# Two transformer models on one core: the passages between projections reordered, two weight units freed earlier, a mixer's last branch in other PSUM banks

## The chip, the core and the metric

The kernel runs on one core of a Trainium2 chip. A core has four compute engines with an instruction queue each: TensorE (PE: matmuls and transposes, results in PSUM), VectorE (DVE), ScalarE (ACT) and GpSimd (POOL); SyncE (SP) issues most transfers. Each queue is in order: an instruction that waits holds back all behind it. The metric is the device time of one execution in microseconds (us), the median over several runs.

## The reference

256 tokens of width 1024 go through two layers of a first model (a mixer with four branches, a layer norm, then a dense feed-forward net in layer 0 and eight experts in layer 1, a layer norm), and then through two layers of a second model (RMS norm, attention in two kinds, RMS norm, SwiGLU, with shifts, scales and gates that come from a conditioning vector). Cut to what matters:

```python
for layer in range(2):                       # first model
    p_swa, p_rwkv, p_fox, p_dsa, p_gate = split_cols(x @ w_in, IN_GROUPS)
    ...
    for i, (o, w) in enumerate(zip((o_swa, o_rwkv, o_fox, o_dsa), w_rows)):
        merged = merged + sigmoid(gate_i) * (o @ w)
    x = layer_norm(ALPHA * x + merged @ w_out, g0, b0)
    y = swiglu(x, w1, w3, w2)  if layer == 0 else  moe_ffn(x, router_w, ...)
    x = layer_norm(ALPHA * x + y, g1, b1)
for l in range(2):                           # second model
    sh_a, sc_a, g_a, sh_f, sc_f, g_f = split(silu(c) @ w_mod[l] + b_mod[l])
    h = rms_norm(x, norm_mix[l]) * (1 + sc_a) + sh_a
    x = x + g_a * (attention(h @ w_in[l]) @ w_out[l])
    h = rms_norm(x, norm_ffn[l]) * (1 + sc_f) + sh_f
    x = x + g_f * ((silu(h @ w_gate[l]) * (h @ w_up[l])) @ w_down[l])
```

All of it is float32.

## The kernel before, in words

The tokens lie in two tiles t of 128. A float32 product is made of three matmuls in a reduced format (fp32r): each operand is split into a high part (a cast, on ACT) and a low part (the rest, a subtraction on DVE), and high·high, high·low and low·high are added in PSUM.

**Weights.** `Stream` brings every weight once, in program order, in units of up to 512 KB. SP issues the transfer of a unit into a raw buffer (L107; 4 of these, 9 from the experts on); `pump` casts one unit's high part on ACT (`wh`, L125) and, one unit later, subtracts its low part on DVE (`wl`, L114). There are 6 pairs of `wh` and `wl`; a new unit may be cast once fewer than 6 are unreleased, and `W.dn` counts those released. `take(n)` hands out the next n units, `W.done()` releases all that have been handed out.

**Order.** The order of each engine is fixed when the program is built. Background generators (transfers of constants, the modulation rows from `w_mod`, which ACT scales at L1709 and POOL adds) are interleaved by a model clock at each `tick`.

**PSUM.** Four banks are named `acc`, four `sm`. `out_proj` takes the four `acc` banks for its sums (two tiles t, two halves n of 512 columns). It goes through the nk units of the weight, both tiles for each; the last `tail` units are held together, all of them first for t=0, then for t=1, so that the first tile's sums end early. `mixer` calls it with 8 units and the default tail of 5; the second model's attention has tail 4 of its own.

**A mixer's last branch** (nb == 4): for each of four column groups c the branch product goes into an `acc` bank, DVE multiplies it by the gate and adds it up (L935, L936), ACT casts the high part `mh` (L940) and DVE subtracts the low part `ml` (L941). `mh` and `ml` are what `out_proj` multiplies by `w_out`.

**A passage** is what lies between the end of one projection and the start of the next: the residual update on the sums in PSUM, the norm, and the turn: 8 transposes of each tile on PE (L340) into `sm` banks, 4 high casts on ACT (L704) and 4 low subtractions on DVE (L744 for t=0, L750 for t=1) of each tile. `normed_T` writes it. A norm consists of `part` (update and statistics of one half, L2112 and L660, or L2219, L2220, L688 and ACT's L681), `stats`, `scale` and `shift` (L668 and L671 for the layer norm; the RMS norm's shift, L691, with a wait for POOL). For the RMS norm (`early`) the order is: t=0's sums, t=1's first half, t=0's shift and turn, t=1's second half, t=0's low parts, t=1's shift and turn, t=1's low parts. `mid` is a start on the next projection with the first tile alone, between the two tiles' transposes; it is used ahead of both attentions of the second model (r=0 and r=6) and both mixers. There are seven passages with a norm: after mixer 0, after the dense net, after mixer 1, after the experts (r=0, where the last layer norm is joined with the first RMS norm), and r=3, r=6 and r=9 in the second model.

## Time and profile before

| | us |
|---|---|
| median of 3 runs (2001.23 to 2015.73) | 2003.49 |
| the profiled execution | 2003.65 |
| its span in the trace | 2001.8 |
| PE busy | 1832.4 (92%) |
| DVE busy | 1446.5 (72%) |
| ACT busy | 1170.8 (58%) |

The granted clock of TensorE was 0.96 of full speed in the mean. In the page's 40 slices of some 50 us PE is busy 0.9 or more in most; it has 0.5 in the slice from about 1250 us, and 0.7 in those from 0, 300, 800, 1400 and 1750 us. A row of a timeline gives the start, the duration, the engine, the line and the operation; what stands in brackets is the time that the engine was idle before it, and what ended that idle time. PE's matmuls are pipelined, so a matmul's duration is longer than its distance to the next one.

### The profile page before, as it was taken

What the parts mean: (1) busy time and instruction counts of PE and PEld (TensorE: products, weight loads), DVE (VectorE), ACT (ScalarE), POOL (GpSimd) and SP (SyncE); (2) the same over time, 40 slices, a digit from 0 to 9 for tenths busy, and PEclk for the clock granted to TensorE, in tenths of its full rate; (3) what the DMA queues carried; (4) which work ended last, traced back from release to release, by engine and by line L of the source; (5) the groups of instructions that cost most, each with busy time, mean ns of one, the idle gap of its engine ahead of it and who ended that gap; (6) DMA issues with size and microseconds to landing.
All of it is one profiled execution on the core that took longest, in us unless ns stands there. A gap on an engine that the chain in (4) does not pass through costs nothing. (4 is left out here: it accounts for less than half of the span.)

```text
span 2001.8 us, 31995 instructions
## 1 busy us (share of the span) xinstructions
PE 1832.4 (92%) x11703; PEld 1625.0 (81%) x11703; DVE 1446.5 (72%) x2255; ACT 1170.8 (58%) x1875; POOL 468.0 (23%) x345
## 2 busy tenths in 40 slices
PE   7999987998899999799999999598799888978998
PEld 7899977987698999588888888486698876768998
DVE  5886776666688656788888888777566758857554
ACT  4465744666465564377777777366466655746443
POOL 0110252777530100100000000111246765113000
PEclk9999988999999999889999999798899998989999
DMA  7553575787864444679999999655378785436662
GB/s 218 152 155 106 173 250 186 261 278 243 268 179 140 136 127 137 208 237 334 365 326 352 327 353 354 233 190 161 76 267 281 253 305 191 148 126 210 196 194 95
DMA packets 287071, 440.08 MB, mean 220 GB/s; under 512 B 31764, under 2 KB 178304, under 8 KB 286904
## 3 DMA queue, kind: packets, MB, share of 16 engines
q1 hardware_dynamic: 281960, 428.29, 64.6%
q0 software_dynamic: 2912, 8.59, 1.6%
q8 instruction: 94, 1.54, 0.3%
q10 hardware_dynamic: 2032, 1.06, 0.2%
q14 instruction: 73, 0.60, 0.1%
HBM read 427.60 MB, written 9.75 MB: 218 GB/s over the span
## 5 line engine op out<-in xcount | busy, mean ns | idle before, releaser
L114 DVE TENSOR_TENSOR wl<-raw,wh 128x1024 fp32r<-128x1024 f32 (+2 forms) x694 | 875.9, 1303 | 175.5 <-ACT wh L125 170.5
L125 ACT CAST wh<-raw 128x1024 fp32r<-128x1024 f32 (+2 forms) x694 | 695.4, 1030 | 201.4 <-PE sm L336 61.0
L336 PE MATMUL acc<-wh,b 128*128 128x512 f32 (+1 forms) x1232 | 417.2, 408 | 22.3 <-DVE b L935 10.5
L336 PE MATMUL sm<-b,wh 128*128 128x256 f32 x2112 | 378.1, 283 | 0.9 <-ACT wh L125 0.9
L336 PE MATMUL acc<-b,wh 128*128 128x256 f32 x2048 | 368.2, 283 | 0.2 <-DVE b L416 0.2
L1711 POOL TENSOR_TENSOR b<-b,b 128x512 f32<-128x512 f32 x168 | 309.8, 1844 | 228.5 <-ACT b L1709 215.5
L336 PE MATMUL sm<-wh,b 128*128 128x512 f32 (+1 forms) x1120 | 342.0, 382 | 0.0
L336 PE MATMUL sm<-b,wl 128*128 128x256 f32 x1056 | 302.2, 286 | 38.2 <-DVE wl L114 38.2
L336 PEld LDWEIGHTS sm<-b,wh 128*128 128x128 f32 x2112 | 332.1, 194 | 4.8 <-ACT wh L125 1.4
L336 PEld LDWEIGHTS acc<-b,wh 128*128 128x128 f32 x2048 | 312.5, 189 | 8.7 <-issue 7.3
L336 PEld LDWEIGHTS acc<-wh,b 128*128 128x128 f32 x1232 | 240.5, 196 | 82.2 <-DVE b L935 13.6
L336 PE MATMUL acc<-b,wl 128*128 128x256 f32 x1024 | 286.1, 279 | 3.0 <-DVE wl L114 3.0
L336 PE MATMUL acc<-wl,b 128*128 128x512 f32 (+1 forms) x616 | 248.6, 404 | 4.3 <-DVE wl L114 4.3
L336 PEld LDWEIGHTS sm<-b,wl 128*128 128x128 f32 x1056 | 205.4, 195 | 44.7 <-DVE wl L114 44.6
L336 PEld LDWEIGHTS sm<-wh,b 128*128 128x128 f32 x1120 | 209.8, 189 | 35.0 <-issue 0.2
L1709 ACT ACTIVATE b<-b,ccol 128x512 f32<-128x512 f32 x192 | 137.4, 724 | 151.8 <-DMA b<-in_w_mod_dram 151.8
L336 PE MATMUL sm<-wl,b 128*128 128x512 f32 (+1 forms) x560 | 213.5, 381 | 0.0
L336 PEld LDWEIGHTS acc<-b,wl 128*128 128x128 f32 x1024 | 193.5, 189 | 3.6 <-DVE wl L114 3.6
L336 PEld LDWEIGHTS acc<-wl,b 128*128 128x128 f32 x616 | 120.8, 196 | 30.5 <-DVE wl L114 7.5
L553 POOL TENSOR_TENSOR ln_mv<-ln_mv,mhalf 128x1 f32<-128x1 f32 x8 | 7.5, 932 | 525.4 <-DVE ln_mv L664 525.4
L336 PEld LDWEIGHTS sm<-wl,b 128*128 128x128 f32 x560 | 105.9, 189 | 18.2 <-DVE wl L114 0.5
L340 PE MATMUL sm<-ident,b 128*128 128x128 f32 (+1 forms) x242 | 46.9, 339 | 72.6 <-DVE b L691 32.1
(333 smaller groups left out, 1738.7 us busy)
## 6 DMA issues: line engine op xcount, KB each, us to landing
raw<-in_exp_w_dram SPq DMA_DIRECT2D x216, 512.0 KB
raw<-in_w_in_dram SPq DMA_DIRECT2D x152, 512.0 KB
b<-in_w_mod_dram SPq DMA_DIRECT2D x192, 256.0 KB
raw<-in_ffn_w_dram SPq DMA_DIRECT2D x66, 512.0 KB
raw<-in_exp_w_dram SPq DMA_DIRECT2D x64, 384.0 KB
raw<-in_w_gate_dram SPq DMA_DIRECT2D x44, 512.0 KB
raw<-in_w_up_dram SPq DMA_DIRECT2D x44, 512.0 KB
raw<-in_w_down_dram SPq DMA_DIRECT2D x44, 512.0 KB
```

The source lines that it names most:

```text
L114: self.K.nc.vector.tensor_sub(*self.lows.pop())
L125: nc.scalar.copy(wh[:, :w], raw[:, :w])
L336: return self.nc.tensor.matmul(out, lhsT, rhs, start=start, stop=stop)
L340: r = self.nc.tensor.transpose(out, in_, ident)
L553: self.nc.gpsimd.tensor_tensor(ap, ap, self.mhalf[:, :n], op=OP.pow)
L1709: nc.scalar.activation(r, r, AF.Copy, scale=cc[:, k : k + 1])
L1711: nc.gpsimd.tensor_add(w["a"], w["a"], r)
```

## The change

- In a mixer's last branch the product goes into `sm` banks, and `ml` of a column group is issued one group later (`last`).
- `out_proj`'s default tail is 4. During t=1's pass over the tail, after the unit at `tail - 3`, two units are declared released (`W.dn = W.ti - 2`) and `pump` casts one more; the same ahead of the last `ffn_down` of a feed-forward net.
- `normed_T`: sums and statistics of both tiles come first. For the RMS norm the shifts of t=0 and t=1 both stand behind t=1's sums; for the layer norm t=0's shift stays ahead of t=1's sums. All eight low parts come after both tiles' turns. `turn` is parted into `turn` (transposes) and `high`.
- At r=0 the joined norm uses the same order, and `mid` is left out there; it stays at r=6 and, with 456 columns, ahead of the mixers.

```diff
--- before.py
+++ after.py
@@ -612,7 +612,7 @@
                 self.tick()
         return ps
 
-    def out_proj(self, aT, nk, tail=5, split_at=None):
+    def out_proj(self, aT, nk, tail=4, split_at=None):
 
         ps = [[self.acc() for _ in range(2)] for _ in range(NT)]
 
@@ -640,6 +640,9 @@
                 part(t, nk - tail + j, w)
                 if t == 0:
                     self.tick()
+                elif j == tail - 3:
+                    self.W.dn = self.W.ti - 2
+                    self.W.pump()
             for n in range(2):
                 for j, w in enumerate(ws[-2:]):
                     part(t, nk - 2 + j, w, (n,))
@@ -692,13 +695,19 @@
 
         return part, stats, scale, shift
 
-    def turn(self, xT, x, t, lows):
+    def turn(self, x):
+
+        r = []
+        for g in range(2):
+            r.append(self.sm().rearrange("p (a b) -> p a b", a=4))
+            for j in range(4):
+                self.tr(r[g][:, j], x[g][:, j * P : (j + 1) * P], self.ident)
+        return r
+
+    def high(self, xT, pss, t, lows):
 
         sl = (slice(None), slice(None), slice(t * P, (t + 1) * P))
-        for g in range(2):
-            ps = self.sm().rearrange("p (a b) -> p a b", a=4)
-            for j in range(4):
-                self.tr(ps[:, j], x[g][:, j * P : (j + 1) * P], self.ident)
+        for g, ps in enumerate(pss):
             for a in range(2):
                 hi, lo = xT[0][2 * g + a][sl], xT[1][2 * g + a][sl]
                 self.nc.scalar.copy(hi, ps[:, 2 * a : 2 * a + 2])
@@ -707,46 +716,39 @@
     def normed_T(self, src, norm=None, early=False, mid=None):
 
 
+
         nc = self.nc
         xT = self.new_xT()
-        lows = ([], [])
+        lows = []
         rest = None
         if norm:
             part, stats, scale, shift = norm
-            for n in range(2):
-                part(0, n)
-                if early:
-                    scale(0, n)
-            stats(0)
+            for t in range(NT):
+                for n in range(2):
+                    part(t, n)
+                    if early and not t:
+                        scale(t, n)
+                if early and t:
+                    for n in range(2):
+                        scale(t, n)
+                stats(t)
+                if not early:
+                    for n in range(2):
+                        scale(t, n)
+                if not early and t == 0:
+                    for n in range(2):
+                        shift(t, n)
             if early:
-                part(1, 0)
-            else:
                 for n in range(2):
-                    scale(0, n)
-            for n in range(2):
-                shift(0, n)
-        self.turn(xT, src[0], 0, lows[0])
-        if mid:
-            rest = mid(xT)
-        if norm:
-            if early:
-                scale(1, 0)
-            else:
-                part(1, 0)
-            part(1, 1)
-            if early:
-                scale(1, 1)
-            stats(1)
-            if not early:
-                for n in range(2):
-                    scale(1, n)
-        for o in lows[0]:
-            nc.vector.tensor_sub(*o)
+                    shift(0, n)
+        self.high(xT, self.turn(src[0]), 0, lows)
         if norm:
             for n in range(2):
                 shift(1, n)
-        self.turn(xT, src[1], 1, lows[1])
-        for o in lows[1]:
+        if mid:
+            rest = mid(xT)
+        self.high(xT, self.turn(src[1]), 1, lows)
+        for o in lows:
             nc.vector.tensor_sub(*o)
         return (xT, rest) if mid else xT
 
@@ -917,8 +919,9 @@
             nb += 1
             rows = range(off[b], off[b + 1])
             ws = self.W.take(len(rows))
+            last = None
             for c in range(4):
-                ps = self.acc().rearrange("p (a b) -> p a b", a=2)
+                ps = (self.acc() if nb < 4 else self.sm()).rearrange("p (a b) -> p a b", a=2)
                 for j in range(2):
                     s = slice(c * 256 + j * P, c * 256 + (j + 1) * P)
                     for r, (wh, wl) in zip(rows, ws):
@@ -938,8 +941,14 @@
                     mh.append(self.b2(dt=F32R))
                     ml.append(self.b2(dt=F32R))
                     nc.scalar.mul(mh[c], mt[c], 0.5)
-                    nc.vector.scalar_tensor_tensor(ml[c], mt[c], 0.5, mh[c], op0=OP.mult, op1=OP.subtract)
-                    del mt[c]
+                    if last:
+                        last()
+
+                    def last(c=c, m=mt.pop(c)):
+                        nc.vector.scalar_tensor_tensor(ml[c], m, 0.5, mh[c], op0=OP.mult, op1=OP.subtract)
+
+            if last:
+                last()
             for r in sorted({r // 2 for r in rows}):
                 oh.d.pop(r), ol.d.pop(r)
         self.phase("w_out")
@@ -1342,6 +1351,8 @@
                 self.ffn_down(y, hid.pop(p - 1), self.W.take(2), p == 1, True)
         ws = self.W.take(4)
         self.ffn_down(y, hid.pop(np_ - 2), ws[:2], False, False)
+        self.W.dn = self.W.ti - 2
+        self.W.pump()
         self.ffn_down(y, hid.pop(np_ - 1), ws[2:], False, False, True)
         self.W.done()
         return y
@@ -2166,23 +2177,18 @@
                 hs = [[self.b2((P, 512)) for _ in range(2)] for _ in range(NT)]
                 part, stats, scale, shift = self.rms_norm(x, hs, update, pre["rows"])
                 if r == 0:
-                    def between(t, n, part=part, scale=scale):
-                        if t == 0:
-                            part(t, n)
-                        elif n == 0:
+                    def late(t, n, part=part, scale=scale):
+                        if t == 1 and n == 0:
                             for m in range(2):
                                 ln[2](1, m)
-
-                    def late(t, n, part=part, scale=scale):
-                        if t == 1:
-                            part(t, n)
-                        scale(t, n)
-
-                    norm = between, stats, late, shift
+                        part(t, n)
+
+                    norm = late, stats, scale, shift
                 else:
                     norm = part, stats, scale, shift
-                xT = self.normed_T(hs, norm, True, self.nat_start(512) if half == 0 else None)
-                if half == 0:
+                xT = self.normed_T(hs, norm, True, self.nat_start(512) if r == 6 else None)
+                begun = None
+                if r == 6:
                     xT, begun = xT
                 for t in range(NT):
                     self.store_x(xd, x, t)
```

The engines' new order is what the diff doesn't show. In the changed kernel the lines are shifted: L935, L936, L940 and L941 are L938, L939, L943 and L948; L2112 is L2123; L660 is L663; L2219 and L2220 are L2225 and L2226; the RMS norm's L688, L684 and L691 are L691, L687 and L694; L744 and L750 are one line, L752.

DVE, last branch of mixer 0, column groups c=0 to 2, before (`b_613` and `b_620` are `ml` of c=0 and c=1, `wl_3385` and `wl_3414` low parts of `w_out`'s units):

```order
L935 SCALAR_TENSOR_TENSOR b_550_2970<-b_550_2970,acc_3371 128x512
L936 TENSOR_TENSOR b_393_2144<-b_393_2144,b_550_2970 128x512
L941 SCALAR_TENSOR_TENSOR b_613_3397<-b_393_2144,b_612_3396 128x512
L114 TENSOR_TENSOR wl_3385<-raw_3253,wh_3384 128x1024
L935 SCALAR_TENSOR_TENSOR b_562_3049<-b_562_3049,acc_3400 128x512
L936 TENSOR_TENSOR b_402_2186<-b_402_2186,b_562_3049 128x512
L941 SCALAR_TENSOR_TENSOR b_620_3426<-b_402_2186,b_619_3425 128x512
L114 TENSOR_TENSOR wl_3414<-raw_3293,wh_3413 128x1024
L935 SCALAR_TENSOR_TENSOR b_579_3155<-b_579_3155,acc_3429 128x512
```

and now:

```order
L938 SCALAR_TENSOR_TENSOR b_550_2970<-b_550_2970,sm_3371 128x512
L939 TENSOR_TENSOR b_393_2144<-b_393_2144,b_550_2970 128x512
L114 TENSOR_TENSOR wl_3385<-raw_3253,wh_3384 128x1024
L938 SCALAR_TENSOR_TENSOR b_562_3049<-b_562_3049,sm_3399 128x512
L939 TENSOR_TENSOR b_402_2186<-b_402_2186,b_562_3049 128x512
L948 SCALAR_TENSOR_TENSOR b_613_3397<-b_393_2144,b_612_3396 128x512
L114 TENSOR_TENSOR wl_3413<-raw_3293,wh_3412 128x1024
L938 SCALAR_TENSOR_TENSOR b_579_3155<-b_579_3155,sm_3428 128x512
L939 TENSOR_TENSOR b_406_2206<-b_406_2206,b_579_3155 128x512
L948 SCALAR_TENSOR_TENSOR b_620_3425<-b_402_2186,b_619_3424 128x512
```

The low part of c=0 moved from behind its own sums, ahead of a weight's low part, to behind the sums of c=1; the reads are from `sm` banks.

DVE, ahead of the first layer norm, from the low part of a `w_out` unit to the first tile's update and statistics, before (`wl_3575` is the last unit of `w_out`):

```order
L114 TENSOR_TENSOR wl_3537<-raw_3417,wh_3536 128x1024
L114 TENSOR_TENSOR wl_3559<-raw_3446,wh_3558 128x1024
L114 TENSOR_TENSOR wl_3575<-raw_3505,wh_3574 128x1024
L2112 SCALAR_TENSOR_TENSOR b_631_3475<-b_631_3475,acc_3491 128x512
L660 BN_STATS ln_bs_3654<-b_631_3475 128x6
L2112 SCALAR_TENSOR_TENSOR b_632_3476<-b_632_3476,acc_3492 128x512
```

and now (`wl_3577` is the last unit of `w_out`):

```order
L114 TENSOR_TENSOR wl_3577<-raw_3505,wh_3576 128x1024
L114 TENSOR_TENSOR wl_3599<-raw_3532,wh_3598 128x1024
L114 TENSOR_TENSOR wl_3608<-raw_3553,wh_3607 128x1024
L2123 SCALAR_TENSOR_TENSOR b_631_3475<-b_631_3475,acc_3491 128x512
L663 BN_STATS ln_bs_3664<-b_631_3475 128x6
L2123 SCALAR_TENSOR_TENSOR b_632_3476<-b_632_3476,acc_3492 128x512
L663 BN_STATS ln_bs_3664<-b_632_3476 128x6
```

Two low parts of the next net's units (`wl_3599`, `wl_3608`) stand ahead of the first tile's update.

DVE in the passage r=3, from the first tile's shift to the second's, before (L691 is the shift, L744 the first tile's low parts):

```order
L691 SCALAR_TENSOR_TENSOR b_4305_19275<-b_4305_19275,rms_st_19279,rw_18986 128x512
L691 SCALAR_TENSOR_TENSOR b_4306_19276<-b_4306_19276,rms_st_19279,rw_18987 128x512
L688 TENSOR_TENSOR b_4307_19277<-b_4234_18972,rw_18982 128x512
L2219 TENSOR_TENSOR b_4324_19322<-acc_18993,b_4237_18979 128x512
L2220 TENSOR_TENSOR b_4235_18973<-b_4235_18973,b_4324_19322 128x512
L688 TENSOR_TENSOR b_4308_19278<-b_4235_18973,rw_18983 128x512
L684 SCALAR_TENSOR_TENSOR rms_st_19280<-rms_st_19280 128x1
L744 TENSOR_TENSOR b_4315_19285<-sm_19307,b_4311_19281 128x2x128
L744 TENSOR_TENSOR b_4316_19286<-sm_19307,b_4312_19282 128x2x128
L744 TENSOR_TENSOR b_4317_19287<-sm_19314,b_4313_19283 128x2x128
L744 TENSOR_TENSOR b_4318_19288<-sm_19314,b_4314_19284 128x2x128
L691 SCALAR_TENSOR_TENSOR b_4307_19277<-b_4307_19277,rms_st_19280,rw_18986 128x512
```

and now, from t=1's residual on (L694 is the shift):

```order
L2226 TENSOR_TENSOR b_4234_18972<-b_4234_18972,b_4324_19307 128x512
L2225 TENSOR_TENSOR b_4325_19311<-acc_18993,b_4237_18979 128x512
L2226 TENSOR_TENSOR b_4235_18973<-b_4235_18973,b_4325_19311 128x512
L691 TENSOR_TENSOR b_4310_19283<-b_4234_18972,rw_18982 128x512
L691 TENSOR_TENSOR b_4311_19284<-b_4235_18973,rw_18983 128x512
L687 SCALAR_TENSOR_TENSOR rms_st_19286<-rms_st_19286 128x1
L694 SCALAR_TENSOR_TENSOR b_4308_19281<-b_4308_19281,rms_st_19285,rw_18986 128x512
L694 SCALAR_TENSOR_TENSOR b_4309_19282<-b_4309_19282,rms_st_19285,rw_18987 128x512
L694 SCALAR_TENSOR_TENSOR b_4310_19283<-b_4310_19283,rms_st_19286,rw_18986 128x512
L694 SCALAR_TENSOR_TENSOR b_4311_19284<-b_4311_19284,rms_st_19286,rw_18987 128x512
L752 TENSOR_TENSOR b_4318_19291<-sm_19321,b_4314_19287 128x2x128
```

The first tile's shift moved from ahead of the second tile's last sums to behind them, and no low part stands between the two tiles' shifts.

## Rows read from the trace of the kernel before

**Rows 1.** page, part 1: engine, busy us (share of the span), instructions
```profile
PE 1832.4 (92%) x11703; PEld 1625.0 (81%) x11703; DVE 1446.5 (72%) x2255; ACT 1170.8 (58%) x1875; POOL 468.0 (23%) x345
```

**Rows 2.** waits of PE: who waited for whom, us in total, times, longest
```profile
PE sm L340 <- DVE b L691: 32.1, 8, 13.1
PE sm L340 <- DVE b L671: 14.6, 4, 5.0
...
PE acc L336 <- DVE b L935: 10.5, 6, 3.3
```

**Rows 3.** timeline of DVE, last branch: start us, us, engine, line, operation [idle before]
```profile
270.27 0.67 DVE L935 SCALAR_TENSOR_TENSOR b<-b,acc 128x512 f32<-128x512 f32 x1
270.98 0.69 DVE L936 TENSOR_TENSOR b<-b,b 128x512 f32<-128x512 f32 x1
272.37 0.69 DVE L941 SCALAR_TENSOR_TENSOR b<-b,b 128x512 fp32r<-128x512 f32 x1 [0.70 <-ACT b L940]
272.98 1.22 DVE L114 TENSOR_TENSOR wl<-raw,wh 128x1024 fp32r<-128x1024 f32 x1
```

**Rows 4.** timeline of PE, same columns, from that branch to the first LN's end
```profile
279.12 0.80 PE L336 MATMUL acc<-wh,b 128*128 128x512 f32 x1 [3.30 <-DVE b L935]
...
311.14 1.97 PE L340 MATMUL sm<-ident,b 128*128 128x128 f32 x8 [4.38 <-DVE b L671]
...
315.77 0.58 PE L336 MATMUL sm<-b,wl 128*128 128x256 f32 x1 [2.45 <-DVE wl L114]
```

**Rows 5.** timeline of ACT, same columns, in the first mixer's w_out
```profile
291.37 0.73 ACT L1709 ACTIVATE b<-b,ccol 128x512 f32<-128x512 f32 x1 [4.56 <-DMA b<-in_w_mod_dram]
```

**Rows 6.** timeline of SP, same columns: the queue that issues the transfers
```profile
285.10 0.33 SPq L107 DMA_DIRECT2D raw<-in_w_out_dram  x1
```

**Rows 7.** timeline of DVE from w_out's last lows to the first LN's second shift
```profile
293.06 3.80 DVE L114 TENSOR_TENSOR wl<-raw,wh 128x1024 fp32r<-128x1024 f32 x2 [4.08 <-ACT wh L125]
297.68 0.69 DVE L2112 SCALAR_TENSOR_TENSOR b<-b,acc 128x512 f32<-128x512 f32 x1 [0.82 <-PE acc L336]
...
304.55 0.69 DVE L2112 SCALAR_TENSOR_TENSOR b<-b,acc 128x512 f32<-128x512 f32 x1 [1.00 <-PE acc L336]
...
309.01 1.41 DVE L744 TENSOR_TENSOR b<-sm,b 128x256 fp32r<-128x256 f32 x4
310.34 1.41 DVE L671 SCALAR_TENSOR_TENSOR b<-b,ln_mv,b 128x512 f32<-128x512 f32 x2
```

**Rows 8.** windows: stretch, us, PE PEld DVE ACT POOL busy, PEclk, DMA share, GB/s
```profile
284.00:297.00 13.00, 12.24 (x48) 9.56 (x47) 8.70 (x6) 8.17 (x12) 6.95 (x4) 0.89 1.00 329
1276.80:1293.90 17.10, 5.70 (x16) 4.03 (x16) 13.46 (x23) 5.37 (x12) 2.47 (x3) 0.50 0.88 305
1437.20:1444.10 6.90, 3.86 (x17) 3.58 (x17) 5.45 (x13) 3.25 (x8) 6.08 (x12) 0.51 0.60 159
```

**Rows 9.** timeline of ACT at the second mixer's w_out
```profile
818.57 0.25 ACT L415 CAST rt_wh<-rt_w 128x64 fp32r<-128x64 f32 x1 [5.63 <-DMA rt_w<-in_router_w_dram]
```

**Rows 10.** timeline of DVE in the passage after the experts (r=0)
```profile
1285.16 1.41 DVE L691 SCALAR_TENSOR_TENSOR b<-b,rms_st,rw 128x512 f32<-128x512 f32 x2
...
1291.94 0.75 DVE L671 SCALAR_TENSOR_TENSOR b<-b,ln_mv,b 128x512 f32<-128x512 f32 x1
...
1296.26 1.41 DVE L691 SCALAR_TENSOR_TENSOR b<-b,rms_st,rw 128x512 f32<-128x512 f32 x2
```

**Rows 11.** timeline of PE in the same passage, both tiles' transposes
```profile
1286.06 1.94 PE L340 MATMUL sm<-ident,b 128*128 128x128 f32 x8 [13.09 <-DVE b L691]
...
1297.06 1.80 PE L340 MATMUL sm<-ident,b 128*128 128x128 f32 x8 [2.90 <-DVE b L691]
```

**Rows 12.** page, part 5: costliest groups: busy us, mean ns | idle before
```profile
L125 ACT CAST wh<-raw 128x1024 fp32r<-128x1024 f32 (+2 forms) x694 | 695.4, 1030 | 201.4 <-PE sm L336 61.0
```

**Rows 13.** timeline of PE in the passage r=3, second transposes and first projection
```profile
1440.07 1.94 PE L340 MATMUL sm<-ident,b 128*128 128x128 f32 x8 [4.24 <-DVE b L691]
...
1444.66 0.39 PE L336 MATMUL sm<-b,wl 128*128 128x256 f32 x1 [0.74 <-DVE wl L114]
```

## The prediction

> **What bounds the kernel now.** I read the page's busy times first: PE is busy 92% of the span, DVE 72%, ACT 58% [rows 1], so PE sets the time wherever it is fed, and only what makes PE wait, or lets its clock fall, can be won. The list of PE's waits says where: transposes that wait for DVE's shift, 32.1 us at the RMS norms and 14.6 us at the layer norms, and the branch products that wait for DVE to empty an `acc` bank, 10.5 us [rows 2]. Together that is 57 us, all of it at the places of the change. The timelines of DVE and PE at these places then show what DVE does in that time, and the windows with the granted clock show what PE does after it: 17.1 us at half speed around the long wait at r=0, 6.9 us after the shorter one at r=3 [rows 8].
>
> **Mixer 0 and its layer norm.** Four column groups cost DVE one `ml` each, and each of these waits 0.70 us for ACT [rows 3]. With `ml` one group later the four waits go: 4 x 0.70 = 2.8 us off the end of the last `ml`. The first `ml` moves the other way: it now stands behind a weight's low part (1.22), a sum (0.67) and an addition (0.69), less the wait of 0.70 [rows 3], so 1.9 us later. `out_proj` needs it in its third matmul, and PE waits there. This wait takes the place of the one for the bank, 3.30 us [rows 4], which the `sm` banks remove; I count the two, with the smaller bank waits, as part of the 2.8 and not again.
>
> What follows is a chain through the transfers. SP issues `w_out`'s last unit at 285.10 [rows 6], when DVE's low part behind the last `ml` has freed its raw buffer; 2.8 us earlier is the most. ACT then stands 4.56 us at a transfer of `w_mod` until 291.37 [rows 5], the two last casts behind it, and the low parts end at 293.06 + 3.80 = 296.86 [rows 7]. If all of it moves by 2.8 us, they end at 294.1. Then come the two new low parts, 2 x 1.22 = 2.4, so t=0's update starts at 296.5 and not at 297.68 [rows 7]. A tile takes 304.55 - 297.68 less the idle 1.00, that is 5.87 us [rows 7]; t=1's update starts at 302.4, 2.2 us earlier. The shorter tail lets PE keep up: six matmuls fewer stand behind the last unit. Behind t=1's sums, t=0's low parts go from between (310.34 - 309.01 = 1.33) [rows 7], and the wait of 2.45 us for a weight at the first matmul of the net goes [rows 4], since that weight is now ready. Sum: 2.2 + 1.3 + 2.45 = **-6.0**. The first term hangs on transfers: the DMA engines are busy all of 284 to 297, at 329 GB/s [rows 8], and the two units are 1 MB more, an estimate of 3.2 us at that rate. With nothing won there and the new low parts in full, it is +2.4 + 0.0 - 3.8 = -1.4; with the whole idle time of the transposes, 4.38 [rows 4], in place of the 2.2, it is -8.1.
>
> **The dense net's passage.** Only the low parts leave the path, 1.33 as in [rows 7], and one weight's low part comes ahead: **-1.5**, from -0.5 to -3.
>
> **Mixer 1 and its layer norm.** The same edits, but ACT waits 5.63 us for the router's weights until 818.57 [rows 9], and `w_out`'s casts are behind it. The transfer of these comes from SP behind the norm's rows and hangs little on `ml`, so what the four groups win is waited away there. What is left: the low parts, 1.33, and the tail. In 284 to 297 PE had 48 matmuls in 12.24 us [rows 8], 0.255 each; six fewer are 1.5, of which the two new low parts on DVE take some: I take 1.0. **-2.3**, from 0 to -5.
>
> **r=0.** Before, 1296.26 - 1285.16 = 11.1 us lie between the two tiles' shifts [rows 10], because two low parts for `mid` stand between. Now t=1's scale and part come ahead: from 1291.94 to 1296.26, less the low parts 1.33, is 3.0 us, so t=0's shift starts at 1288.2, t=1's 1.3 later at 1289.5. The second tile is ready 6.8 us earlier, but the eight matmuls of `mid`, done in the gap before, are still to do, the first weights are cast only behind the eight high parts on ACT, and the clock is low until 1293.9 [rows 8]. I place the projection's start at 1295: shift and transposes end by 1289.5 + 1.4 + 1.9 = 1292.8 [rows 10, 11], then come a cast (1.03) [rows 12] and a low part (1.22) [rows 3]. Before, the eight matmuls were done by the end of the second transposes, 1297.06 + 1.80 = 1298.9 [rows 11], and the high parts came behind that. Now they are still to do from 1295 on: 0.255 us each at a clock of 0.89 [rows 8] is 0.45 at half speed, 3.6 for the eight, so PE is at the same state at 1298.6. That is -0.3, and with the high parts done earlier as well I take **-1.0**, from +1 to -3.
>
> **r=3 and r=9.** They repeat each other to a tenth of a us. t=1's transposes at 1440.07 [rows 13] follow a shift that loses the low parts ahead of it, 1.33 as in [rows 7], and the wait of 0.74 for a weight [rows 13] goes, as one more is ready: -2.0. Against it, t=0's transposes now come directly ahead of t=1's, at half speed 1.94 for the eight [rows 13], and ACT has all eight high parts in a row: +0.4. **-1.6 each**, from -0.5 to -2.5.
>
> What the row shows here is a PE that waits 4.24 us [rows 13] between two short bursts and is then at half speed for 6.9 us [rows 8]. The Trainium skill, "TensorE: Matmul & The Clock Gate", section "HAM oscillation — how this bites in real kernels", says that idle gaps in PE's work should be kept short, since a long one drops the clock and every return to work is then paid at half rate again. This change makes one idle stretch out of two, which that rule speaks against. By the rule the two places would cost some us and not win them, by the rows, where the clock was low there already, they win 1.6 each.
>
> **r=6.** `mid` stays. One weight's low part, 1.22 as in [rows 3], and t=0's low parts, 1.33 as in [rows 7], leave the way of t=1's shift: -2.5. But t=0's transposes, and `mid` behind them, wait for t=1's sums, and t=1's transposes stand behind `mid` on PE. **-0.7**, from +1.5 to -2.5.
>
> **The rest** of the program keeps its order; at its start there is no norm and at its end no turn. Sum: 6.0 + 1.5 + 2.3 + 1.0 + 2 x 1.6 + 0.7 = 14.7 us. Against the profiled execution, 2003.65 (span 2001.8 and 1.85 around it), that is 1988.95. The profiled execution lies 0.16 above the median of the runs shown, so the forecast is **1989**.
>
> **Rivals.** *Weights late.* The units freed early land too late, and DVE, in order, stands at their low parts with the first tile's update behind them. For it speaks the DMA share of 1.00 [rows 8]; against it, that they come right behind `w_out`'s last unit in SP's queue. It costs the first term of mixer 0 and 1.0 at mixer 1: 14.7 - 4.6 - 1.0 = 9, so 1995.
>
> *Clock.* With the waits shorter, PE stays at full speed through more of the passages. Each stretch of 6.9 us [rows 8] that vanishes gives back half; four of them, at r=3, r=6, r=9 and one layer norm, are 14 more: 1975. Against it, at the RMS norms the idle time becomes one piece, and that no shorter by much than the 4.24 us of before [rows 13].
>
> *Slower.* At the RMS norms t=0's transposes wait for t=1's sums, and PE stands idle in one piece. If PE then stays low as long as at r=0, 17.1 and not 6.9 us [rows 8], r=3, r=6 and r=9 lose half of 10.2 each, 15.3, and the wait for the first `ml` comes on top, 2 x 1.9: 1989 + 19 = 2008. The gain is gone once these passages together stay at half speed for 29 us more (2 x 14.7). Against it: the wait of 13.09 us that went ahead there [rows 11] is three times as long as the 4.24 at r=3 [rows 13]. The rule of the Trainium skill named above ("TensorE: Matmul & The Clock Gate", "HAM oscillation — how this bites in real kernels") would make this the likelier outcome.
>
> **The numbers.** About 1% (20 us) is what a measurement of this kernel can tell from no change: faster means below 1983.5, slower above 2023.5. The forecast case (1981 to 1996) has 0.55; weights late, 0.20; the clock, 0.15; slower, 0.10. From the best ends of the forecast's terms and the clock case comes the low end, 1975; the high end takes in weights late with the passages' poor ends, 2001. Below it lie some 0.08, above it 0.10. Faster by over 1%: 0.14 of the clock case and 0.16 of the forecast's, whose terms' best ends together reach 1977, so 0.30. Slower by over 1% needs the slower case with more than its worked-out price: 0.06. Within 1%: 0.64.
>
> **What would show it.** In the changed kernel's profile: no wait of PE for DVE's product in the last branches, and one of about 1.9 us for the first `ml`; t=1's shift at r=3 and r=9 directly behind t=0's; no wait for a weight at the first matmul after mixer 0's norm, r=3 and r=9; the router's wait unchanged. The prediction is wrong if the first tile's update after mixer 0 starts later than before, if the half-speed stretches at r=3 and r=9 get much longer or vanish, or if the stage behind r=3, where ACT waits for `w_mod`, takes its gain back.

## The result and the profile after

The changed kernel takes 1983.32 us (median of 5 runs, 1982.3 to 1988.47), the kernel before 2005.3 us in the runs beside it: a ratio of 0.989, interval 0.9858 to 0.9922, so 22 us less. Of the five runs of the kernel before one, 2111.68 us, was a slow one, and the ratio leaves it out. The forecast was 1989, the range 1975 to 2001; against the 2003.49 us of the forecast's table the time lies just beyond the 1% bound, on the faster side. The profiled execution has a span of 1981.4 us, 20.4 less than before's.

The page's first part after, to be held against [rows 1], and PE's waits (who for whom, us in total, times, longest) against [rows 2]; L694 is the old L691, L674 the old L671, L948 the last branch's `ml`:

```profile
PE 1819.1 (92%) x11703; PEld 1618.3 (82%) x11703; DVE 1449.0 (73%) x2255; ACT 1169.1 (59%) x1875; POOL 471.0 (24%) x345
```

```profile
PE sm L340 <- DVE b L694: 30.9, 4, 16.1
...
PE sm L340 <- DVE b L674: 12.3, 4, 4.3
...
PE acc L336 <- DVE b L948: 2.5, 2, 1.6
```

The reader is to see two things. The same 11703 matmuls keep PE busy for 13.3 us less than in [rows 1]. That is not less work: summed over the stretches of low clock, PE was busy at half speed for 98 us and not 119, which accounts for some 10 of the 13.3, and only some 7 of the 20.4 us are idle time. How a gain divides between the two hangs on the execution: pin_all below, as fast in its profiled run (1982.74 us), has PE busy for 1826.7 us, 110 of them at half speed. And the list of waits hardly shows the gain: the RMS norms wait 30.9 us in four pieces in place of 32.1 in eight.

Mixer 0's tail and its norm. DVE (start, duration, operation, idle before), against [rows 3] and [rows 7]:

```profile
270.16 0.68 DVE L938 SCALAR_TENSOR_TENSOR b<-b,sm 128x512 f32<-128x512 f32 x1
...
273.94 0.69 DVE L948 SCALAR_TENSOR_TENSOR b<-b,b 128x512 fp32r<-128x512 f32 x1
...
280.03 1.47 DVE L948 SCALAR_TENSOR_TENSOR b<-b,b 128x512 fp32r<-128x512 f32 x2
...
291.82 1.53 DVE L114 TENSOR_TENSOR wl<-raw,wh 128x1024 fp32r<-128x1024 f32 x1 [4.07 <-ACT wh L125]
...
296.79 0.68 DVE L2123 SCALAR_TENSOR_TENSOR b<-b,acc 128x512 f32<-128x512 f32 x1
...
302.51 0.68 DVE L2123 SCALAR_TENSOR_TENSOR b<-b,acc 128x512 f32<-128x512 f32 x1
...
308.23 2.73 DVE L752 TENSOR_TENSOR b<-sm,b 128x256 fp32r<-128x256 f32 x8
```

ACT there, against [rows 5]:

```profile
290.13 0.72 ACT L1720 ACTIVATE b<-b,ccol 128x512 f32<-128x512 f32 x1 [4.77 <-DMA b<-in_w_mod_dram]
```

PE there, against [rows 4]:

```profile
274.68 0.73 PE L336 MATMUL acc<-wh,b 128*128 128x512 f32 x2 [1.63 <-DVE b L948]
...
291.84 0.49 PE L336 MATMUL acc<-wh,b 128*128 128x512 f32 x1 [2.46 <-ACT wh L125]
293.40 0.51 PE L336 MATMUL acc<-wl,b 128*128 128x512 f32 x1 [1.07 <-DVE wl L114]
...
307.79 1.69 PE L340 MATMUL sm<-ident,b 128*128 128x128 f32 x8 [4.31 <-DVE b L674]
```

The first `ml` is waited for 1.63 us (1.9 forecast), the last unit's low part ends at 293.35 (294.1), the first tile's update starts at 296.79 (296.5) and the second's at 302.51 (302.4). No weight is waited for at the net's first matmul.

One link is off. ACT's wait for `w_mod` ends at 290.13 for 291.37, 1.24 us earlier and not 2.8. The low parts end early all the same because only one of `w_out`'s, and not two as in [rows 7], stands behind that wait. And at `w_out`'s last unit PE waits 2.46 + 1.07 us, where it waited 0.76 before:

```profile
296.91 0.50 PE L336 MATMUL acc<-wl,b 128*128 128x512 f32 x1 [0.76 <-DVE wl L114]
```

The passages r=0, r=3 and r=6 on PE, against [rows 11] and [rows 13]:

```profile
1272.01 3.65 PE L340 MATMUL sm<-ident,b 128*128 128x128 f32 x16 [16.05 <-DVE b L694]
...
1420.60 3.46 PE L340 MATMUL sm<-ident,b 128*128 128x128 f32 x16 [3.54 <-DVE b L694]
...
1647.40 1.97 PE L340 MATMUL sm<-ident,b 128*128 128x128 f32 x8 [7.78 <-DVE b L694]
```

Before, the first tile's transposes at r=3, and both tiles' at r=6, were:

```profile
1434.54 1.29 PE L340 MATMUL sm<-ident,b 128*128 128x128 f32 x8 [0.89 <-DVE b L691]
...
1663.93 1.38 PE L340 MATMUL sm<-ident,b 128*128 128x128 f32 x8 [2.49 <-DVE b L691]
...
1670.60 1.97 PE L340 MATMUL sm<-ident,b 128*128 128x128 f32 x8 [3.43 <-DVE b L691]
```

At r=3 one wait of 3.54 us stands where 0.89, 4.24 and 0.74 stood. Windows of the changed kernel with the granted clock (us, busy times, clock, DMA share, GB/s), against [rows 8]:

```profile
1260.40:1284.30 23.90, 10.14 (x30) 8.02 (x31) 22.82 (x39) 11.69 (x23) 5.60 (x8) 0.50 0.86 300
1420.80:1424.30 3.50, 3.50 (x19) 3.34 (x18) 3.40 (x9) 2.15 (x7) 3.50 (x8) 0.51 0.62 225
```

The low stretch at r=3 is 3.5 us and not 6.9, but PE's busy time in it is 3.50 and not 3.86 [rows 8]; at r=0 it is 23.9 and not 17.1 and 3.4.

### The profile page after: what moved, and what is told of

Read it like the earlier page. It is cut to its first block, busy times and chain, and to the rows that moved or that the text cites. A ratio compares the mean times of both kernels' runs of the same rounds, so it can differ in the third digit from the quotient of the medians.

```text
span 1981.4 us, 32010 instructions
## 1 busy us (share of the span) xinstructions
PE 1819.1 (92%) x11703; PEld 1618.3 (82%) x11703; DVE 1449.0 (73%) x2255; ACT 1169.1 (59%) x1875; POOL 471.0 (24%) x345
## 3 DMA queue, kind: packets, MB, share of 16 engines
q10 hardware_dynamic: 2032, 1.06, 0.2%
## 5 line engine op out<-in xcount | busy, mean ns | idle before, releaser
L336 PE MATMUL sm<-b,wh 128*128 128x256 f32 x2176 | 384.8, 281 | 2.0 <-ACT wh L125 2.0
L336 PE MATMUL acc<-b,wh 128*128 128x256 f32 x1984 | 357.1, 283 | 0.2 <-DVE b L416 0.2
L336 PEld LDWEIGHTS sm<-b,wh 128*128 128x128 f32 x2176 | 338.0, 192 | 5.9 <-ACT wh L125 2.8
L336 PE MATMUL sm<-b,wl 128*128 128x256 f32 x1088 | 308.3, 284 | 34.0 <-DVE wl L114 33.8
L336 PEld LDWEIGHTS acc<-b,wh 128*128 128x128 f32 x1984 | 303.0, 189 | 8.7 <-issue 7.0
L336 PE MATMUL acc<-b,wl 128*128 128x256 f32 x992 | 277.1, 279 | 2.3 <-DVE wl L114 2.3
L336 PEld LDWEIGHTS acc<-b,wl 128*128 128x128 f32 x992 | 187.4, 189 | 2.7 <-DVE wl L114 2.7
L340 PE MATMUL sm<-ident,b 128*128 128x128 f32 (+1 forms) x242 | 46.6, 341 | 71.3 <-DVE b L694 30.9
```

What stands on the lines that cost most here:

```text
L336: return self.nc.tensor.matmul(out, lhsT, rhs, start=start, stop=stop)
L340: r = self.nc.tensor.transpose(out, in_, ident)
```

## The experiments

Three parts are told apart: **free** (tail 4, early release), **branch** (`sm` banks, `ml` later) and **order** (`normed_T`, r=0). All ratios are to the kernel before on the same chip, with their 95% interval.

| run | ratio | interval |
|---|---|---|
| changed kernel | 0.989 | 0.9858 to 0.9922 |
| order_only | 0.9988 | 0.9971 to 1.0004 |
| branch_only | 0.9974 | 0.9958 to 0.9989 |
| free_only | 0.9886 | 0.9868 to 0.9904 |
| plan_free | 0.992 | 0.9905 to 0.9934 |
| pin_free | 0.9933 | 0.9916 to 0.995 |
| pin_free_branch | 0.9934 | 0.9909 to 0.9959 |
| pin_free_order | 0.9906 | 0.9875 to 0.9937 |
| pin_all | 0.9884 | 0.9867 to 0.9902 |
| after_planfree | 0.9847 | 0.9829 to 0.9865 |
| warm | 0.9956 | 0.994 to 0.9973 |
| dense | 0.9867 | 0.984 to 0.9893 |
| best | 0.9817 | 0.9794 to 0.9841 |

**One part alone.** order_only is the changed kernel with the other two parts taken back:

```diff
-    def out_proj(self, aT, nk, tail=4, split_at=None):
+    def out_proj(self, aT, nk, tail=5, split_at=None):
...
-                elif j == tail - 3:
-                    self.W.dn = self.W.ti - 2
-                    self.W.pump()
...
-                ps = (self.acc() if nb < 4 else self.sm()).rearrange("p (a b) -> p a b", a=2)
+                ps = self.acc().rearrange("p (a b) -> p a b", a=2)
```

> The kernel before with only normed_T's new order and r=0's joined norm without mid; tail 5, no early release, last branch as before. Theory of starts (the prediction's terms): it is worth the low parts taken off the path, 1.3 us at each of three layer norms, about 0.9 at r=3 and r=9, 1.0 at r=0, 0.7 at r=6, so 7.5 us, 0.996 of before. Theory of the clock: most of the gain is that PE's idle time at a passage gets short enough for the granted clock to stay up or come back sooner, and the order does that; then 12 us or more, 0.994 or less, with PE busy time down by 6 us or more. Rival (the units freed early carry it): 0.998 to 1.0, since the wait for a weight takes what the order wins.

branch_only and free_only are the kernel before with these lines alone (free_only also with the two lines ahead of the last `ffn_down`):

```diff
-                ps = self.acc().rearrange("p (a b) -> p a b", a=2)
+                ps = (self.acc() if nb < 4 else self.sm()).rearrange("p (a b) -> p a b", a=2)
...
+                    if last:
+                        last()
```

> The kernel before with only the mixers' last branch in sm banks and ml one column group later. Theory of starts: 2.8 us come off each last ml, of which the transfers let some 2 through in mixer 0 and none in mixer 1 (router's weights): 2 to 3 us, 0.9985. Theory of the clock: PE loses its 10.5 us of bank waits and with them the half-speed stretches of 10 us at mixer 0 and 7 us at mixer 1; PE busy falls by 5 us or more, but what is won before the out projection is given back at its last units unless these come earlier too.

```diff
-    def out_proj(self, aT, nk, tail=5, split_at=None):
+    def out_proj(self, aT, nk, tail=4, split_at=None):
...
+                elif j == tail - 3:
+                    self.W.dn = self.W.ti - 2
+                    self.W.pump()
```

> The kernel before with only tail 4 and the early release of two units with one pump. Theory of starts: the waits for a weight behind the passages go (2.45 at mixer 0, 0.74 at r=3 and at r=9) and the shorter tail is worth 1 us per mixer: 5 to 6 us, 0.997. Rival (weights late): two low parts stand ahead of the first tile's update and the passage starts 2.4 us later at both mixers: 0.999 to 1.002.

Measured: the order alone is worth nothing that can be told, as the rival in its expectation had it; the branch 5 us, somewhat more than the 2 to 3 expected, which its interval takes in; the early release alone 23 us, as much as the whole change and far beyond its expectation. The traces showed why one should not read this as "free is the change": free_only wins in mixer 1's gates and in the last attention, which it doesn't touch. The model clock, which sees other casts at other times, had put background steps elsewhere: of PE's 1935 instructions that are not products with a weight, 769 stand elsewhere among the weight products than before, 679 of them by more than a dozen. In the changed kernel it is 89 and 17.

The zero of order_only is no clean reading either, since 137 rows stand elsewhere there. In its profiled run the passages are 11.5 us shorter than before, and the stages between 13 us longer; half of that is the last attention, where PE is idle for 16.9 us and not 11.2:

```profile
1756.32 1.09 PE L340 MATMUL sm<-ident,b 128*128 128x128 f32 x4 [4.69 <-DVE b L1887]
```

**The planner held fixed.** So the choices of the model clock were recorded (which background step comes at each `tick`, how many units are cast by then) and replayed:

```diff
     def tick(self, mark=None):
+        e = self.script()
+        if e is not None:
+            self.play(e)
+            return
         self.feed()
...
+    def play(self, e):
+        while self.W and self.W.si < e[0]:
+            at = self.W.si
+            self.W.pump()
+            if self.W.si == at:
+                break
+        for name, o in e[1]:
+            c = [b for b in self.bgs if b.name == name]
+            if o < len(c):
+                self.advance(c[o])
```

pin_free is free_only with the choices of before; plan_free is before with the choices of free_only; pin_all is the changed kernel with those of before; after_planfree is the changed kernel with those of free_only.

> The early release and tail 4 alone, but with every choice of the model clock (when a weight unit is cast, which background step comes next) replayed as the kernel before made it, so that PE, SP and POOL have the order of before and only a few casts and low parts move. Theory of the planner: the 23 us of the early release alone come from the background work that the model clock then places elsewhere (mixer 1's gates, the last attention); pinned, only the prediction's terms are left, 5 to 6 us, 0.996 to 0.998 of before. Theory of the direct effect: units that are ready earlier are worth the 23 us, 0.987 to 0.990.

> The kernel before with none of the three edits, but with the choices of the model clock replayed as the kernel with the early release alone made them: only background work moves. Theory of the planner: 0.990 to 0.993, won in mixer 1's gates and the last attention and not in the passages. Theory of the direct effect: 0.999 to 1.001.

> The whole change with the choices of the model clock replayed from the kernel before. Its stages in the traces so far: the passages win 24 us against the profiled run of before and the stages between lose 4. If the passages are the direct effect, 0.987 to 0.990, as the changed kernel; if the changed kernel's gain needs its own background order too, 0.993 to 0.997; by the prediction's terms alone (14.7 us) 0.9927.

> The changed kernel with the choices of the model clock replayed from the kernel with the early release alone. Theory of the planner: the passages' gain and the background's gain add up, 0.979 to 0.983 of before, faster than both. If both roads end at the same bound (weights and modulation rows arrive no earlier), 0.987 to 0.990.

free_only falls apart into two effects of some 13 us (pin_free, between its two theories) and 16 us (plan_free, as the planner's theory had it). They don't simply add up: their sum is 29 us, free_only's gain 23. What carries the 13 us, where the forecast's terms gave 5 to 6, is not known.

The whole change with before's background is worth as much as with its own (0.9884 and 0.989, as a direct effect of the passages had it), so its own background order wins nothing that can be told; with free_only's it is faster still, 0.9847, between the two theories, and that interval lies clear of pin_all's. In the pinned runs PE's order is that of the kernel whose choices are replayed: none of those rows stands more than a dozen weight products from its place there.

The time between the same matmuls of the program in these traces, less that in the trace of before, us:

| stage (us in before) | changed | pin_all | pin_free | plan_free | after_planfree |
|---|---|---|---|---|---|
| mixer 0's end, norm (265 to 350) | -9.8 | -2.6 | -2.6 | -5.7 | -6.0 |
| dense net's passage (522 to 570) | -5.0 | -5.4 | -3.3 | -1.3 | -3.8 |
| mixer 1 (570 to 805) | -0.2 | -1.2 | -0.1 | -5.6 | -4.8 |
| its end, norm, router (805 to 870) | -4.0 | -8.0 | -3.3 | 0.0 | -2.5 |
| r=0 (1270 to 1310) | +0.3 | -0.1 | +0.2 | 0.0 | -1.2 |
| r=3 (1431 to 1448) | -3.1 | -3.1 | -0.8 | +0.1 | -2.6 |
| net behind r=3 (1448 to 1633) | -1.0 | -3.3 | -2.1 | -7.0 | -3.4 |
| r=6 (1633 to 1687) | +0.3 | +0.2 | -1.0 | +0.8 | +0.1 |
| last attention (1687 to 1804) | +3.3 | +2.3 | +0.3 | -5.6 | -3.8 |
| r=9 (1804 to 1820) | -2.9 | -2.9 | -0.6 | +2.0 | -2.7 |

One execution each: where the clock happens to be low moves a stage by several us. Ahead of 265 us pin_free has before's order on PE, and is 2.5 us longer there, with PE busy at half speed for 9.1 us and not 2.8. The four stretches that the table leaves out lose 2.2, 3.4, 8.7, 6.4 and 2.4 us in its columns' order, most of it ahead of 265 and from 350 to 522; so pin_free's profiled run, at the slow end of its runs, is only 5.0 us shorter than before's, where its ratio says 13. In mixer 0's stage the changed kernel and pin_all differ by 7.2 us, some 5 of them from PE's time at half speed, 9.7 us more of it in pin_all; they also differ in order there, since with before's choices two low parts of `w_out` stand behind ACT's wait and not one. The steadiest stages are r=3 and r=9, the latter but for plan_free, where the clock fell.

In the last attention the background order of free_only takes a wait away. PE's transposes of the attention's output waited for DVE 13.5 us before; in after_planfree, where that line is L2033 since the replay's code shifts the lines:

```profile
PE sm L340 <- DVE b L1923: 13.5, 5, 3.7
```

```profile
PE sm L392 <- DVE b L2033: 6.4, 2, 3.7
```

The two waits that are left are those of the attention before it.

**What the branch and the order add, the planner fixed.** Both are pin_free with one more part of the change's diff.

```diff
-                ps = self.acc().rearrange("p (a b) -> p a b", a=2)
+                ps = (self.acc() if nb < 4 else self.sm()).rearrange("p (a b) -> p a b", a=2)
```

> Early release, tail 4 and the last branch in sm banks, normed_T as before, the model clock's choices replayed from the kernel before. So far, all replayed: the early release alone 0.9933 of before, the whole change 0.9884. If the branch carries the rest, 0.989; if the order does, 0.993; by the prediction's terms the order's share is the larger (7.5 us of low parts against some 4), so 0.991 to 0.992.

```diff
-        self.turn(xT, src[0], 0, lows[0])
...
+        self.high(xT, self.turn(src[0]), 0, lows)
```

> Early release, tail 4 and normed_T's new order (with r=0's), the mixers' last branch as before, the model clock's choices replayed from the kernel before. If the order carries the rest, 0.9885; if it wins nothing without the branch, 0.993. The stages r=3 and r=9 hold no branch: in the traces they win 0.8 and 0.6 us with the early release alone, 1.3 each with the order alone, 3.1 and 2.9 with both, so there the order must show its full share: 0.9895 to 0.991.

The branch adds nothing that can be told to the early release (0.9934 beside 0.9933; the interval leaves room for 5 us either way). The traces show why at mixer 0. In pin_free PE waits 1.23 + 3.30 + 1.06 us for banks and then 0.91 at `w_out`'s last units, 6.5 in all:

```profile
281.14 0.80 PE L387 MATMUL acc<-wh,b 128*128 128x512 f32 x1 [3.30 <-DVE b L1033]
...
299.42 0.50 PE L387 MATMUL acc<-wl,b 128*128 128x512 f32 x1 [0.91 <-DVE wl L114]
```

In pin_free_branch it waits 1.67 us for the first `ml` and then 3.34 + 0.76 + 0.57 at the last units, 6.3 in all:

```profile
274.68 0.72 PE L387 MATMUL acc<-wh,b 128*128 128x512 f32 x2 [1.67 <-DVE b L1044]
...
292.06 0.80 PE L387 MATMUL acc<-wh,b 128*128 128x512 f32 x1 [3.34 <-ACT wh L125]
```

What the branch wins ahead of `w_out` is given back at its last units, as the expectation of branch_only had it for the case that these come no earlier. The order's 0.9906 lies between; the whole change, 0.9884, is told clearly from the early release alone, but the interval of pin_free_order reaches over both, so how much of these 10 us the order carries without the branch stays open. At r=3 and r=9 its trace wins 3.0 and 2.9 us, as much as the whole change.

**The clock.** In warm and dense PE gets matmuls whose result is never read, in the place of its wait at the passages; the rest keeps its order, but for 23 of the 1935 rows counted above.

```diff
+    def warm(self, us):
+        if us:
+            at = self.clock
+            ps = self.sm()
+            for _ in range(round(us / 0.08)):
+                self.mm(ps[:, :P], self.identr, self.onesr, True, True)
+            self.clock = at
...
+        if early:
+            self.warm(fill)
         self.high(xT, self.turn(src[0]), 0, lows)
+        if not early:
+            self.warm(fill)
```

> The changed kernel with filler matmuls (constant operands, 128 columns, result never read) on PE ahead of the transposes it waits for: 15 to 32 at the layer norms, 156 at r=0, 22 at r=3 and r=9, 62 at r=6; every other instruction in the same order. Theory of the clock: the half-speed stretches of the passages go; with PE busy in about 10 us of the low stretch at r=0, 5 at r=6 and nearly all of 3.4 at each of the five others, half of it is won: 10 to 16 us, 0.981 to 0.984 of before. Rival: the clock behind a passage costs little because PE is waiting for weights there anyway: within 3 us of the changed kernel, 0.988 to 0.990. If fillers run past the wait they are sized for, the transposes start later and it is slower than the changed kernel.

In dense the operands are the next weight unit, 512 columns:

```diff
-                self.mm(ps[:, :P], self.identr, self.onesr, True, True)
+            self.mm(ps, w[:, 0, :P], x, True, True)
...
+                                   {0: 0, 3: 13, 6: 24, 9: 13}[r])
```

> The changed kernel with filler matmuls whose operands are a weight unit that lies ready (512 columns, at the dense net's norm 456; result never read), 16, 10 and 15 at the layer norms, 13 at r=3 and r=9, 24 at r=6, none at r=0, sized by the waits of the changed kernel at 0.227 us each; all other instructions in the same order. Theory of the clock: the low stretches behind these waits go, 3.4 us at each of the norms and 10 at r=6, half of PE's busy time in them: 8 to 12 us against the changed kernel, 0.983 to 0.985 of before. Rival: within 3 us of it, 0.9875 to 0.9905, since the fillers take the place of idle time only and PE waits for weights soon after.

warm was slower than the changed kernel, and the row says where: its 156 fillers at r=0 took 33.35 us, and the wait that they were to fill was 16.05. That is the case of fillers that run past their wait, which the expectation names.

```profile
1257.88 33.35 PE L336 MATMUL sm<-onesr,identr 128*128 128x128 f32 x156 [3.35 <-DVEq L1671]
```

dense has r=3 at full clock from end to end. The window of 16 us there, of the changed kernel and of dense:

```profile
1414.00:1430.00 16.00, 12.46 (x83) 11.45 (x82) 14.60 (x26) 9.89 (x22) 7.47 (x13) 0.89 0.44 75
```

```profile
1414.00:1430.00 16.00, 15.27 (x112) 13.48 (x112) 15.26 (x25) 10.76 (x19) 6.93 (x12) 1.00 0.56 116
```

The clock is 1.00 and not 0.89, and the transposes take 2.62 us there and not 3.46:

```profile
1418.22 2.62 PE L340 MATMUL sm<-ident,b 128*128 128x128 f32 x16 [0.59 <-DVE b L694]
```

By the stages, dense wins a further 0.8 us at r=3, 1.0 at r=9, 2.6 at the dense net's passage and 2.5 at r=6, where the low stretch of 10 us is gone, and loses 2.4 in the net behind r=3; in all the expected 8 to 12 us became some 3 to 5, and the interval overlaps the changed kernel's. That the clock costs something in the passages is shown there; that it is most of what is left is not.

**best** is after_planfree with the fillers of dense (the two diffs above together).

> The changed kernel with the choices of the model clock replayed from the kernel with the early release alone, and the fillers of the run dense at the same places. Alone, the replay gave 0.9847 of before and the fillers 0.9867, against 0.989 for the changed kernel. If the two add up, 0.980 to 0.9835; if the fillers win nothing here, since the waits at the layer norms fall otherwise, 0.984 to 0.986.

It is 1971.95 us, 36 us below before, and faster than the changed kernel with intervals clear of each other, as the case in which the two gains add up had it. That the fillers win something on top of after_planfree is not told for itself: these two intervals overlap (0.9794 to 0.9841 and 0.9829 to 0.9865).

## Why the prediction was right, and where it was not

**The sum.** The seven passages won 24.2 us in the changed kernel's profiled run and 21.9 in pin_all's, where 14.7 were forecast; the stages between lost some 4 and 1. So the places were right, and several terms were too small.

**Mixer 0.** The stage won 9.8 us in the changed kernel and 2.6 in pin_all, for 6.0 forecast, so its size is not shown by these runs. The end of the low parts, both updates and the new wait for the first `ml` came within 0.8 us of the forecast, but the link through ACT did not hold: the end came out right because one cast had moved ahead of ACT's wait, which is luck. The last `ml` does end earlier, 11.3 us behind the branch's first sum (270.16 to 281.50) and not 13.6 (270.27 to 283.90):

```profile
283.21 0.69 DVE L941 SCALAR_TENSOR_TENSOR b<-b,b 128x512 fp32r<-128x512 f32 x1 [0.70 <-ACT b L940]
```

But ACT's wait for `w_mod` moved by 1.24 us only, and PE gave back at `w_out`'s last units more than half of what it had won ahead of them. The forecast had counted on the transfer to come earlier by as much as `ml`.

**The dense net's passage** was the term most surely mis-sized: 1.5 forecast, with 3 as its best end, 5.0 and 5.4 measured. I counted the first tile's low parts. But a weight's low part had stood between the first tile's shift and the second tile's sums as well, and with both gone PE's waits for the shift there fell from 0.79 and 5.02 us to 1.23 and 2.68. Before, PE and DVE:

```profile
539.35 1.38 PE L340 MATMUL sm<-ident,b 128*128 128x128 f32 x8 [0.79 <-DVE b L671]
...
547.41 1.97 PE L340 MATMUL sm<-ident,b 128*128 128x128 f32 x8 [5.02 <-DVE b L671]
```

```profile
539.87 1.10 DVE L114 TENSOR_TENSOR wl<-raw,wh 128x912 fp32r<-128x912 f32 x1
```

PE in the changed kernel:

```profile
530.59 1.38 PE L340 MATMUL sm<-ident,b 128*128 128x128 f32 x8 [1.23 <-DVE b L674]
...
536.30 1.78 PE L340 MATMUL sm<-ident,b 128*128 128x128 f32 x8 [2.68 <-DVE b L674]
```

That is 1.9 of the 5.0 us. Another 1.5 is idle time in the net's last products, ahead of the norm, and 1.6 is PE's busy time, of which 6.8 us and not 9.2 fell at half speed.

**Mixer 1.** The router's weights bound it as forecast (ACT waits 6.55 us for them, 5.63 in [rows 9]); PE then stands at `w_out`'s low parts:

```profile
803.59 0.24 ACT L415 CAST rt_wh<-rt_w 128x64 fp32r<-128x64 f32 x1 [6.55 <-DMA rt_w<-in_router_w_dram]
```

```profile
805.28 0.80 PE L336 MATMUL acc<-wl,b 128*128 128x512 f32 x1 [4.95 <-DVE wl L114]
```

The stage won 4.0 us for the 2.3 forecast; its idle time is the same, 14.5 for 14.4, and the difference is time at half speed, 16.9 us for 23.8. So the two terms of the forecast, both of them idle time, are not seen here; in pin_all, where the stage won 8.0, idle time is 1.8 of it.

**r=0** came out at +0.3 for -1.0, inside its range: `mid` gone, PE waits 16.05 us in one piece for 13.09 and 2.90, and does the eight matmuls behind it at half speed.

**r=3 and r=9** won 3.1 and 2.9 for 1.6, beyond the 2.5 of the best end. The direction was argued from the right rows, but the +0.4 for the transposes in a row did not show: 0.89 + 4.24 + 0.74 became 3.54, 2.3 us less idle, and PE's busy time fell by another 0.8. Here the rule of the Trainium skill ("TensorE: Matmul & The Clock Gate", "HAM oscillation — how this bites in real kernels") did not decide: the clock fell at the one idle stretch too, but that was shorter than the longer of the two it replaced.

**r=6** gave +0.3 for -0.7: 7.78 us of wait where 2.49 and 3.43 stood; that is inside its range, on the poor side, for the reason given there.

**"The rest of the program keeps its order"** was taken for granted. It came out nearly true of the changed kernel, where 89 of the 1935 rows moved, and before's choices give the same time as its own. It need not have: in free_only, with one of the three parts, 769 moved, and those choices alone are worth 16 us, more than the forecast's whole sum and in none of its terms. That the forecast came out near is in part luck, since the change's own order happened to be neutral.

Of the rivals, *weights late* did not happen in the changed kernel (296.79 for 297.68). With before's background order it did at mixer 0: counted from the branch's first sum the first tile's update starts after 27.4 us before, 26.6 in the changed kernel, 27.7 in pin_all and 29.2 in pin_free, whose rows are these:

```profile
272.30 0.68 DVE L1033 SCALAR_TENSOR_TENSOR b<-b,acc 128x512 f32<-128x512 f32 x1
...
301.53 0.67 DVE L2215 SCALAR_TENSOR_TENSOR b<-b,acc 128x512 f32<-128x512 f32 x1
```

Both are faster than before even so. *Slower* did not happen, since the low stretches behind the waits got shorter at r=3 and r=9. *Clock* did in part: at the mixers and the dense net a share of what the sum missed is time at half speed, which the sum left out and only a rival held. That rival's price was too high: it took half of each 6.9 us, though PE is busy for 3.86 of them [rows 8].

## What to carry to other kernels

Where a planner orders background work by a model of time, an edit of one place moves others: before a gain is put down to an edit, replay the planner's choices with and without it; here that took apart 13 and 16 us, which the plain comparison had shown as one gain of 23, and led to the fastest version. In a passage where PE waits, a term of the sum is worth its idle time and half of the busy time in the low stretch behind it (at r=6 of the changed kernel products of 512 columns start 0.43 us apart at the low clock and 0.23 at the high one); reckon both. A wait that is taken away can come back further on: at mixer 0 the branch's 4 us for banks became 4 us at `w_out`'s last units. And waits that follow one another hide each other: at r=3 the order alone won 1.3 us, the early release 0.8, both together 3.0.

## What the runs showed of the hardware

The clock can stay low while PE is busy without a break. In warm it stayed at the lower level, 1.2 GHz, through all of the 156, and through the transposes and first projections behind them, and rose some 6 us after these had begun:

```profile
1258.00:1291.00 33.00, 33.00 (x156) 33.00 (x157) 13.79 (x26) 2.83 (x8) 5.59 (x8) 0.50 0.49 176
1291.00:1302.00 11.00, 8.85 (x29) 7.01 (x29) 8.70 (x13) 8.26 (x14) 0.00 (x0) 0.50 0.28 90
1302.50:1310.00 7.50, 7.50 (x34) 6.16 (x33) 3.95 (x4) 3.61 (x4) 0.00 (x0) 1.00 1.00 357
```

At r=3 of dense, PE did 13 matmuls on a weight unit at full clock and then waited 0.59 us, and the clock stayed high. What makes the difference between the two was not tried.
